# Splitting the projection weights on POOL alone instead of on ScalarE and VectorE, in a bidirectional hybrid mixer

## The chip, the core and the metric

The kernel runs on one core of one Trainium2 chip. The time is device microseconds of one execution. Of the core's engines, PE (TensorE) multiplies matrices, PEld is its weight load, DVE is VectorE, ACT is ScalarE, POOL is GpSimd, and SP issues most DMAs.

## The reference, cut to what matters

Two layers run over 256 context tokens and 1024 latent tokens, 1024 features wide. In each layer one input projection feeds three head groups, and one output projection closes the layer:

```python
h = _rmsnorm(x, g) * (1.0 + scale) + shift
proj = jnp.einsum('bld,de->ble', h, w_in)              # 4400 columns
(aq, ak, av, ao, az, ag, bq, bk, bv, bz, cq, ck, cv, cz, clr) = split(proj)
ha = mlstm(aq, ak, av, gates ag) both directions        # group A, 4 heads x 128
hb = retention(bq, bk, bv) both directions              # group B, 4 heads x 64
hc = gla(cq, ck, cv, log_a from clr) both directions    # group C, 4 heads, 32 x 64
y = concat(head_rms(sigmoid(ao) * ha), head_rms(hb), head_rms(hc)) * hn_g * silu(concat(az, bz, cz))
x = x + gate * jnp.einsum('ble,ed->bld', y, w_out)
```

All data are float32. The mLSTM's gates `ag` pass through a log-sigmoid, running sums and running maxima over the tokens before anything of group A can use them.

## The kernel before, in words

**Projections.** PE multiplies float32 data as three products of a high part (`hi`, type fp32r) and a rest (`lo`): hi by hi, hi by lo, lo by hi (`TERMS`). The normed activations lie split in `hA` (six chunks of 128 tokens) and `hB` (four chunks), first the high part, then the rest. Each weight tile is 1024 columns by 128 partitions: it lands in one of two `raw` buffers by a DMA of 512 KB, and `split` (L410 to L417) makes `hi` and `lo` of it, each a ring of three buffers. ACT copies raw to `hi` (a cast, L415), and DVE subtracts `hi` from raw into `lo` (L416).

**Two kinds of projection.** `w_fm` takes 128 output features over all 8 slices of the input (its split is one piece of 1024 columns), and `mm_fm` (L454) runs 24 matmuls over each of three token blocks of 256, 512 and 512. `w_tm` takes 256 output features in two weight tiles (each split in four pieces of 256 columns), and `mm_tm` (L466) runs 24 matmuls for each of the ten token chunks, two chunks to one PSUM bank; `pj` has two banks. There are 44 tiles of the first kind and 36 of the second, 16 of them for the output projection. `gates_w` (L508 to L518) makes 6 more tiles for the columns of `cv`, `ag` and `clr`, used by `gates` (L534).

**Order of the work.** `ORDER` names the steps of each layer; all steps are issued in that order, and a list scheduler places every instruction on its engine from its own estimate of when each is ready. Projections carry a low priority (`late`), so they fill the PE's time between the small matmuls of the head groups. On the engine the order is then fixed: an instruction that waits holds up all that stand behind it.

**The start of a layer.** The steps begin with `g` (gates), then `v0`, `cq`, `ck` and `m` in layer 0 and `cq`, `v0`, `ck` and `m` in layer 1. `gates` transposes its results on PE (L543), and ACT adds a bias into `G` (L544). `mlstm_rows` (step `m`, from L546) takes `G` and runs a chain of small operations on 36 partitions, nearly all on DVE: a copy (L554), the log-sigmoid (L207 to L213), 20 running sums (L504), running maxima (L560, L562), subtractions (L568 to L591), and an exponential on ACT (L593). Its result goes back to PE for transposition (L603, then L598). Step `d` (`decays`, matmul L653) and group C (L780 on) follow.

**POOL** does little: the power -1/2 in each head's norm (L619, L1190, L356), some clearing (as L650 in `decays`), a masked copy (L818) and a few of the activations' rests (L401).

Of the kernel before, what the change touches and what calls it, by code (L numbers as in the profile page):

```python
# [10 lines left out]
F32 = mybir.dt.float32  # L11
# [4 lines left out]
ALU = mybir.AluOpType  # L16
# [72 lines left out]
def hybrid_step(ctx: ExitStack, tc: tile.TileContext, A, O):  # L89
    nc = tc.nc  # L90
    pe, dve, act, pool, sync = nc.tensor, nc.vector, nc.scalar, nc.gpsimd, nc.sync
# [41 lines left out]
    def v3(t, n):  # L133

        return t.rearrange("p (a n) -> p a n", n=n)
# [271 lines left out]
            f5.give(*xn)  # L407


    def split(raw, parts=1, cols=1024):  # L410
        hi, lo = hi_ring(), lo_ring()
        n = cols // parts
        for i in range(0, cols, n):
            e = slice(i, i + n)
            act.copy(hi[:, e], raw[:, e])  # L415
            dve.tensor_tensor(lo[:, e], raw[:, e], hi[:, e].bitcast(F32), ALU.subtract)  # L416
        return hi, lo  # L417

    def w_fm(src, c0):

        raw = raw_ring()
        sync.dma_start(v3(raw, P), src[:, c0:c0 + P].rearrange("(k p) n -> p k n", p=P))
        hi, lo = split(raw)
        return v3(hi, P), v3(lo, P)

    def w_tm(src, c0, ks=range(KT)):

        out = []
        for g in range(2):
            raw = raw_ring()  # L430
            i = 0
            while i < 4:
                k = ks[4 * g + i]
                n = 1
                while i + n < 4 and ks[4 * g + i + n] == k + n:
                    n += 1
                sync.dma_start(v3(raw, 256)[:, i:i + n, :],
                               src[k * P:(k + n) * P, c0:c0 + 256].rearrange("(k p) n -> p k n", p=P))
                i += n
            hi, lo = split(raw, 4)  # L440
            out.append((v3(hi, 256), v3(lo, 256)))
        return out
# [34 lines left out]
    def proj_feat(l, c0, scale=None):  # L477
        w = w_fm(A["w_in"][l], c0)
        t = f5()
        for b, (t0, n) in enumerate(BLK):  # L480
            ps = mm_fm(w, b)
            evac(t[:, t0:t0 + n], ps[:, :n], scale)
        return t
# [23 lines left out]
    def gates_w(l):  # L507

        src = A["w_in"][l].rearrange("(k p) n -> p k n", p=P)
        out = []  # L510
        for k in range(0, KT, 3):
            n = min(3, KT - k)
            raw = raw_ring()
            r = v3(raw[:, 0:912], 304)[:, 0:n, :]
            for d, c0, m in ((0, C_CV, 256), (256, C_AG, 16), (272, C_LR, 32)):
                sync.dma_start(r[:, :, d:d + m], src[:, k:k + n, c0:c0 + m])
            hi, lo = split(raw, 1, n * 304)
            out.append((v3(hi[:, 0:912], 304), v3(lo[:, 0:912], 304)))  # L518
        return out

# [677 lines left out]
    def gate_z(l, c0, kt, y=None):  # L1198

        w = w_fm(A["w_in"][l], c0)  # L1200
        for b, (t0, n) in enumerate(BLK):
            ps = mm_fm(w, b)
            th = (wk if y is None else rw)()[:, :n]
            act.activation(th, ps[:, :n], AF.Tanh, scale=0.5)
            dve.scalar_tensor_tensor(th, th, 1.0, ps[:, :n], ALU.add, ALU.mult)
            if y is None:
                yv = wk()[:, :n]
                sync.dma_start(yv, yd[kt, :, t0:t0 + n])
            else:
                yv = y[:, t0:t0 + n]  # L1210
            dve.scalar_tensor_tensor(yv, th, hgh[:, 8 * l + kt:8 * l + kt + 1], yv, ALU.mult, ALU.mult)
            if y is None:
                sync.dma_start(yd[kt, :, t0:t0 + n], yv)


    def layer(l, general, w):
# [7 lines left out]
        def step_g():  # L1224
            e["vc"], e["G"] = anchored(gates, l, gates_w(l) if l or general else w)
# [148 lines left out]
    def program(general):  # L1374
        w = None
        if general:
            for b in range(3):
                norm_h(0, b, load_x(b))
        else:
            halves = range(4), range(4, 8)  # L1380
            units = [f5(1024) for _ in range(6)]
            xn = [load_x(0)]
            modulation_pe(0, units, scz)
            modulation_pe(1024, units, scz)
            with tc.issue_after(adas[-1].ins):
                xn.append(load_x(1))
            for b in range(2):
                norm_h(0, b, xn[b], halves[0])
            modulation_pe(512, units, scz)
            modulation_pe(1536, units, scz)  # L1390
            f5.give(*units)
            with tc.issue_after(adas[-1].ins):
                w = gates_w(0)
                xn.append(load_x(2))
            for b in range(3):
                norm_h(0, b, xn[b], halves[1] if b < 2 else range(KT))
# [53 lines left out]
```

## Time and profile before

| what | value |
| --- | --- |
| median of three runs | 1653.74 us (1653.5 to 1653.74) |
| profiled execution, its own time | 1656.08 us |
| span of its trace | 1654.1 us |
| PE busy | 1588.9 us (96%), 10874 matmuls |
| DVE busy | 984.9 us (60%), 2516 instructions |
| ACT busy | 615.7 us (37%), 1605 instructions |
| POOL busy | 153.1 us (9%), 243 instructions |
| DMA engines, mean over 16 | some 34% of the span |

The profiled execution took 2.0 us more than its span, and 2.3 us more than the median of the timed runs. PE's busy time counts a matmul from its start to its modelled end, and matmuls overlap, so a busy PE can still issue below its peak rate.

### The profile page before, as it was taken

To read this page: it belongs to the slowest core of one execution; us is meant where nothing else is said; L and a number is where in the kernel's file an instruction comes from. 1 tells how busy PE (TensorE), PEld (TensorE's weight loads), DVE (VectorE), ACT (ScalarE), POOL (GpSimd) and SP (SyncE) were. 2 spreads that over 40 slices of the span, in tenths; PEclk is the share of its full clock that TensorE was granted. 3 is DMA by queue.
4 is the path that set the end of the run, shared out by engine and by line. 5 is a ranking of instruction groups with operands and counts; after the bars stand their busy time and mean duration, and the time that the engine had idled before them with its cause. 6 is when DMAs were issued, how large, how long until landed. Compare 5 with 4: busy or idle time off the path is not lost.

```text
span 1654.1 us, 28521 instructions
## 1 busy us (share of the span) xinstructions
PE 1588.9 (96%) x10874; PEld 1430.0 (86%) x10874; DVE 984.9 (60%) x2516; ACT 615.7 (37%) x1605; POOL 153.1 (9%) x243
## 2 busy tenths in 40 slices
PE   6889999999999999999999899999999999899997
PEld 2887879888989998889999777999988989888997
DVE  3576664677779855763455677454537633466545
ACT  5535423434112324342365453244411223434323
POOL 1200221101001101000021012100001100000001
PEclk9998999999999999999999999999999999999999
DMA  9211323544324433561141031423233232435203
GB/s 326 71 41 40 76 66 92 153 144 123 102 82 141 149 111 118 192 187 35 37 160 39 17 87 44 110 84 102 73 96 85 58 93 83 125 105 178 80 13 131
DMA packets 169312, 167.43 MB, mean 101 GB/s; under 512 B 19084, under 2 KB 144940, under 8 KB 169164
## 3 DMA queue, kind: packets, MB, share of 16 engines
q1 hardware_dynamic: 168992, 165.45, 33.5%
q8 instruction: 87, 1.43, 0.4%
q14 instruction: 61, 0.50, 0.1%
q10 hardware_dynamic: 172, 0.05, 0.0%
HBM read 129.49 MB, written 27.85 MB: 95 GB/s over the span
## 4 chain that ended last, share of the span: by engine, by line
PE 81%; DMA 7%; DVE 7%; ACT 3%; issue 1%; SPq 0%; POOL 0%; POOLq 0%; DVEq 0%; ACTq 0%
PE pj L454 32%; PE pj L466 26%; PE pj L534 3%; DMA rw<-rrow 2%; PE mx L827 2%; PE mx L1172 2%; PE mx L1121 2%; PE mx L1174 2%; DMA wk<-yd 1%; DVE f L504 1%; DMA f<-f 1%; PE mx L999 1%; PE mx L1042 1%; PE mx L1163 1%; PE mx L292 1%
## 5 line engine op out<-in xcount | busy, mean ns | idle before, releaser
L454 PE MATMUL pj<-hA,hi 128*128 128x256 f32 (+1 forms) x1408 | 369.4, 345 | 0.1
L466 PE MATMUL pj<-hi,hA 128*128 128x256 f32 x1728 | 343.9, 286 | 6.5 <-ACT f L473 2.4
L466 PEld LDWEIGHTS pj<-hi,hA 128*128 128x128 f32 x1728 | 274.7, 189 | 10.8 <-ACT f L473 3.2
L454 PEld LDWEIGHTS pj<-hA,hi 128*128 128x128 f32 x1408 | 242.2, 189 | 30.7 <-issue 2.3
L466 PE MATMUL pj<-hi,hB 128*128 128x256 f32 x1152 | 248.5, 289 | 6.8 <-ACT f L1087 4.4
L454 PE MATMUL pj<-hA,lo 128*128 128x256 f32 (+1 forms) x704 | 238.5, 343 | 0.5 <-DVE lo L416 0.5
L466 PE MATMUL pj<-lo,hA 128*128 128x256 f32 x864 | 236.6, 285 | 0.0
L454 PE MATMUL pj<-hB,hi 128*128 128x512 f32 x704 | 234.8, 403 | 1.7 <-ACT f L473 0.9
L466 PEld LDWEIGHTS pj<-hi,hB 128*128 128x128 f32 x1152 | 193.5, 192 | 9.6 <-ACT f L1087 4.9
L416 DVE TENSOR_TENSOR lo<-raw,hi 128x256 fp32r<-128x256 f32 (+2 forms) x194 | 119.3, 628 | 101.5 <-ACT hi L415 90.0
L466 PE MATMUL pj<-lo,hB 128*128 128x256 f32 x576 | 165.4, 288 | 0.0
L466 PEld LDWEIGHTS pj<-lo,hA 128*128 128x128 f32 x864 | 159.1, 189 | 0.0
L454 PEld LDWEIGHTS pj<-hB,hi 128*128 128x128 f32 x704 | 129.9, 189 | 33.1 <-issue 4.1
L415 ACT CAST hi<-raw 128x256 fp32r<-128x256 f32 (+2 forms) x194 | 107.5, 566 | 135.9 <-PE pj L454 99.1
L454 PEld LDWEIGHTS pj<-hA,lo 128*128 128x128 f32 x704 | 132.7, 189 | 16.2 <-issue 1.0
L454 PE MATMUL pj<-hB,lo 128*128 128x512 f32 x352 | 140.7, 400 | 0.0
L466 PEld LDWEIGHTS pj<-lo,hB 128*128 128x128 f32 x576 | 110.2, 192 | 0.4 <-issue 0.3
L310 DVE SCALAR_TENSOR_TENSOR f<-f,sc 128x256 f32<-128x256 f32 x224 | 96.1, 480 | 16.5 <-DMA f<-in_w_ada_dram 16.2
L473 ACT COPY f<-pj 128x256 f32<-128x256 f32 (+2 forms) x142 | 48.4, 389 | 103.5 <-PE pj L466 48.0
L351 ACT ACTIVATE rw<-f 128x256 bf16<-128x256 f32 (+1 forms) x90 | 43.3, 482 | 107.7 <-DVE f L1343 102.8
L1156 DVE SCALAR_TENSOR_TENSOR rw<-rw,ccol,cst 128x128 f32<-128x128 f32 x160 | 46.7, 347 | 57.1 <-DMA rw<-rrow 56.9
L454 PEld LDWEIGHTS pj<-hB,lo 128*128 128x128 f32 x352 | 66.4, 189 | 15.4 <-issue 1.3
(282 smaller groups left out, 2546.9 us busy)
## 6 DMA issues: line engine op xcount, KB each, us to landing
raw<-in_w_in_dram SPq DMA_DIRECT2D x64, 512.0 KB
f<-in_w_ada_dram SPq DMA_DIRECT2D x32, 384.0 KB
wk<-yd SPq DMA_DIRECT2D x48, 256.0 KB
rw<-rrow SPq DMA_DIRECT2D x40, 256.0 KB
rw<-wrow SPq DMA_DIRECT2D x40, 256.0 KB
f<-in_w_ada_dram SPq DMA_DIRECT2D x16, 512.0 KB
f<-in_x_sample_dram SPq DMA_DIRECT2D x16, 512.0 KB
raw<-in_w_out_dram SPq DMA_DIRECT2D x32, 256.0 KB
```

Of the source, the lines that this page charges most:

```text
L310: dve.scalar_tensor_tensor(acc[v], w, scv[:, k, v:v + 1], acc[v], ALU.mult, ALU.add)
L351: act.activation(rw().bitcast(BF16)[:, 0:x.shape[1]], x, AF.Square, accum_out=out)
L415: act.copy(hi[:, e], raw[:, e])
L416: dve.tensor_tensor(lo[:, e], raw[:, e], hi[:, e].bitcast(F32), ALU.subtract)
L454: pe.matmul(ps[:, :n], lhsT=w[wi][:, k, :], rhs=hblk(xi, k, b), start=(i == 0), stop=(i == 23))
L466: pe.matmul(pv[:, u, :], lhsT=hchunk(xi, k, c), rhs=w[e // 4][wi][:, e % 4, :], start=(i == 0), stop=(i == 23))
L473: act.copy(out, ps)
L534: pe.matmul(ps, lhsT=hchunk(xi, k, c), rhs=w[k // 3][wi][:, k % 3, :], start=(i == 0), stop=(i == 23))
L827: pe.matmul(sc[d][:, 256 * p:256 * p + 256], lhsT=k[p][h, s], rhs=qm[p][h, :, u, :], start=True, stop=True)
L1121: pe.matmul(U[d], lhsT=ks[:, d * P:(d + 1) * P], rhs=v[:, c, :], start=True, stop=True)
L1156: dve.scalar_tensor_tensor(r4[:, d, e, :], r4[:, d, e, :], ccol[:, c0 + e, d, hd:hd + 1], negm[d], ALU.add, ALU.min)
L1172: pe.matmul(po[:, d, :], lhsT=r4[:, d, e, :], rhs=v[:, c, :], start=True, stop=not inter)
```

## The change

`split` gets a new argument, `own`, which is true unless the caller says otherwise. With it, POOL makes both parts: a cast of raw into `hi` (L417) and the subtraction into `lo` (L418). `w_fm` now splits in four pieces of 256 columns, as `w_tm` did already. Only the six gate tiles of `gates_w` keep ACT and DVE (L420, L421). Five lines are added inside `split`, so every later line of the kernel has a number five higher: L454 becomes L459, L466 becomes L471, L543 becomes L548, L603 becomes L608.

```diff
-    def split(raw, parts=1, cols=1024):
+    def split(raw, parts=1, cols=1024, own=True):
+
         hi, lo = hi_ring(), lo_ring()
         n = cols // parts
         for i in range(0, cols, n):
             e = slice(i, i + n)
-            act.copy(hi[:, e], raw[:, e])
-            dve.tensor_tensor(lo[:, e], raw[:, e], hi[:, e].bitcast(F32), ALU.subtract)
+            if own:
+                pool.tensor_copy(hi[:, e], raw[:, e])
+                pool.tensor_tensor(lo[:, e], raw[:, e], hi[:, e].bitcast(F32), ALU.subtract)
+            else:
+                act.copy(hi[:, e], raw[:, e])
+                dve.tensor_tensor(lo[:, e], raw[:, e], hi[:, e].bitcast(F32), ALU.subtract)
         return hi, lo
...
-        hi, lo = split(raw)
+        hi, lo = split(raw, 4)
...
-            hi, lo = split(raw, 1, n * 304)
+            hi, lo = split(raw, 1, n * 304, own=False)
```

Since the scheduler orders every engine anew, the change also moves instructions that it does not name. On PE, at the start of layer 0, the last transpositions of the gates (L543, into `mx`) and the first matmuls of `v0` (L466) stand like this before, with the first L603 of step `m` at the end:

```order
L543 MATMUL mx_112<-cst,sm_86 128x128
L466 MATMUL pj_110<-hi_66,hA_106 128x256
...
L466 MATMUL pj_110<-hi_66,hA_106 128x256
L543 MATMUL mx_112<-cst,sm_83 128x128
L466 MATMUL pj_111<-hi_66,hA_106 128x256
...
L454 MATMUL pj_111<-hA_107,hi_68 128x256
L603 MATMUL mx_114<-cst,f_99 128x36 x4
```

Of the change, the same place (L548 and L471 are the same two lines, L608 is L603):

```order
L548 MATMUL mx_112<-cst,sm_86 128x128
L471 MATMUL pj_110<-hi_66,hA_106 128x256
L471 MATMUL pj_110<-hi_66,hA_107 128x256
L548 MATMUL mx_112<-cst,sm_83 128x128
L471 MATMUL pj_111<-hi_66,hA_106 128x256
...
L471 MATMUL pj_111<-hi_67,hB_109 128x256
L608 MATMUL mx_114<-cst,f_99 128x36 x4
```

Before, 25 projection matmuls stand between the two transpositions and 203 more (189 of `v0`, 14 of `cq`) ahead of L603. With the change these are 2 and 142, all of `v0`. At the same place of layer 1 the projection matmuls ahead of L603 go from 204 (72 of `cq`, 132 of `v0`) to 127 (72 of `cq`, 55 of `v0`).

On POOL, at the start of layer 0, before, the clearing of the gates' tiles (L539) is followed at once by the clearing of step `d` (L650):

```order
L539 MEMSET sm_86 128x128
L539 MEMSET sm_83 128x128
L650 MEMSET f_105 64x10
L650 MEMSET f_94 64x10 x2
L1099 COPY f_98<-vT 128x1
```

Of the change, the splits of the two tiles of `v0` (`hi_66`, `hi_67`) and of `cq` (`hi_68`) stand between them:

```order
L544 MEMSET sm_86 128x128
L544 MEMSET sm_83 128x128
L417 CAST hi_66<-raw_65 128x256 x4
L418 TENSOR_TENSOR lo_69<-raw_65,hi_66 128x256
L417 CAST hi_67<-raw_64 128x256 x4
L418 TENSOR_TENSOR lo_69<-raw_65,hi_66 128x256 x3
L418 TENSOR_TENSOR lo_70<-raw_64,hi_67 128x256 x4
L417 CAST hi_68<-raw_65 128x256 x4
L418 TENSOR_TENSOR lo_71<-raw_65,hi_68 128x256 x4
L655 MEMSET f_105 64x10
L655 MEMSET f_94 64x10 x2
```

These are 24 new POOL instructions while step `m` runs on DVE; at the same place of layer 1 there are 32 (`cq`, both tiles of `v0`, `ck`).

On DVE, in the chain of step `m` of layer 1, splits (L416) stand between its operations before:

```order
L416 TENSOR_TENSOR lo_71<-raw_64,hi_68 128x256 x2
L554 COPY f_100<-f_105 36x1280
L416 TENSOR_TENSOR lo_71<-raw_64,hi_68 128x256 x2
L207 SCALAR_TENSOR_TENSOR f_98<-f_100 36x1280
L209 TENSOR_SCALAR f_104<-f_98 36x1280
...
L504 SCALAR_TENSOR_TENSOR f_98<-ones,f_100 4x128
L416 TENSOR_TENSOR lo_69<-raw_65,hi_66 128x1024
L504 SCALAR_TENSOR_TENSOR f_98<-ones,f_100 4x128 x5
```

Of the change, the same chain stands without them, and otherwise in the same order:

```order
L405 TENSOR_TENSOR hB_109<-rw_77,hB_108 128x512
L559 COPY f_100<-f_105 36x1280
L207 SCALAR_TENSOR_TENSOR f_98<-f_100 36x1280
L209 TENSOR_SCALAR f_104<-f_98 36x1280
...
L509 SCALAR_TENSOR_TENSOR f_98<-ones,f_100 4x128 x6
```

Before, five splits (four of 256 columns, one of 1024) stand between L554 and the second L504; with the change none does.

## Rows read from the trace of the kernel before

**Rows 1.** The page: busy time by engine, and the chain that ended last.

```profile
PE 1588.9 (96%) x10874; PEld 1430.0 (86%) x10874; DVE 984.9 (60%) x2516; ACT 615.7 (37%) x1605; POOL 153.1 (9%) x243
...
PE 81%; DMA 7%; DVE 7%; ACT 3%; issue 1%; SPq 0%; POOL 0%; POOLq 0%; DVEq 0%; ACTq 0%
```

**Rows 2.** Busy time by stretch: length, PE, PEld, DVE, ACT, POOL, granted clock, DMA.

```profile
100.00:120.00 20.00, 15.91 (x133) 15.50 (x132) 19.67 (x36) 3.99 (x8) 0.00 (x0) 1.00 0.02 3
120.00:134.00 14.00, 14.00 (x52) 10.74 (x52) 1.75 (x12) 6.29 (x9) 0.33 (x3) 0.51 0.04 8
134.00:900.00 766.00, 754.27 (x5175) 682.07 (x5174) 501.89 (x1308) 284.28 (x768) 75.24 (x106) 1.00 0.37 110
930.00:935.00 5.00, 5.00 (x28) 4.93 (x29) 1.20 (x9) 2.33 (x2) 0.11 (x1) 0.50 0.07 12
935.00:1654.00 719.00, 695.37 (x4797) 630.79 (x4796) 386.87 (x1034) 253.04 (x684) 62.02 (x84) 0.99 0.30 89
```

**Rows 3.** PE's waits: total, times, longest, in us.

```profile
PE mx L603 <- ACT f L593: 7.2, 2, 3.7
...
PE pj L454 <- DVE lo L416: 0.5, 1, 0.5
```

**Rows 4.** The page's groups of the splits: busy, mean ns, idle before.

```profile
L416 DVE TENSOR_TENSOR lo<-raw,hi 128x256 fp32r<-128x256 f32 (+2 forms) x194 | 119.3, 628 | 101.5 <-ACT hi L415 90.0
...
L415 ACT CAST hi<-raw 128x256 fp32r<-128x256 f32 (+2 forms) x194 | 107.5, 566 | 135.9 <-PE pj L454 99.1
```

**Rows 5.** The chain in order of time: start, length, a long run of projections.

```profile
1539.64 77.19 PE pj L466 x644
```

**Rows 6.** Layer 0, from the gates to L603: start, length, engine, line.

```profile
86.92 0.22 ACT L542 COPY sm<-pj 128x32 f32<-128x32 f32 x1
...
89.41 0.27 PE L543 MATMUL mx<-cst,sm 128*128 128x128 f32 x1
...
90.28 0.68 ACT L544 ACTIVATE f<-mx,gb 128x512 f32<-128x512 f32 x1
...
90.41 1.23 DVE L416 TENSOR_TENSOR lo<-raw,hi 128x1024 fp32r<-128x1024 f32 x1 [3.57 <-ACT hi L415]
91.67 0.82 DVE L554 COPY f<-f 36x1280 f32<-36x1280 f32 x1
...
119.87 1.11 PE L603 MATMUL mx<-cst,f 36*128 36x36 f32 x10 [3.71 <-ACT f L593]
```

**Rows 7.** Layer 1, the same stretch.

```profile
895.11 0.22 ACT L542 COPY sm<-pj 128x32 f32<-128x32 f32 x1
...
899.72 0.82 DVE L554 COPY f<-f 36x1280 f32<-36x1280 f32 x1
900.58 0.76 DVE L416 TENSOR_TENSOR lo<-raw,hi 128x256 fp32r<-128x256 f32 x2
...
917.85 1.22 DVE L416 TENSOR_TENSOR lo<-raw,hi 128x1024 fp32r<-128x1024 f32 x1
...
929.96 1.28 PE L603 MATMUL mx<-cst,f 36*128 36x36 f32 x10 [3.47 <-ACT f L593]
```

**Rows 8.** POOL's groups nearest to the new ones, shapes apart.

```profile
L818 POOL TENSOR_SCALAR rw<-f,heads_of 128x256 f32<-128x256 f32 x20 | 23.0, 1158 | 81.1 <-DVE f L741 42.3 <-PE mx L827 38.7
...
L401 POOL TENSOR_TENSOR hA<-rw,hA 128x256 fp32r<-128x256 f32 x4 | 3.5, 885 | 22.3 <-ACT hA L400 22.3
...
L674 POOL MEMSET sta<- 128x256 f32 x6 | 1.9, 312 | 5.3 <-DMA out_dram<-sta 2.8 <-issue 1.8 <-POOL nout L1107 0.7
```

**Rows 9.** DVE and POOL beside each other in the timeline from 61.8 us.

```profile
62.23 3.35 DVE L405 TENSOR_TENSOR hB<-rw,hB 128x512 fp32r<-128x512 f32 x2
...
62.04 1.29 POOL L401 TENSOR_TENSOR hB<-rw,hB 128x512 fp32r<-128x512 f32 x1 [8.29 <-ACT hB L400]
...
63.58 1.45 POOL L401 TENSOR_TENSOR hB<-rw,hB 128x512 fp32r<-128x512 f32 x1
```

**Rows 10.** DVE's line L405: durations in ns, least, median, most.

```profile
L405 DVE TENSOR_TENSOR hB<-rw,hB x12: 674/683/1777, 59.6 to 881.6; 128x512 fp32r<-128x512 f32 x12
```

## The prediction

> **What bounds the kernel now.** The page comes first: PE is busy 96% of the span, and 81% of the chain that ended last is PE's own work, with DVE 7%, DMA 7% and ACT 3% [rows 1]. So the 1654.1 us are PE's work plus its idle time, 1654.1 - 1588.9 = 65.2 us. The busy time by stretch says where that idle time lies: 4.1 us in 100 to 120 us, 11.7 us in 134 to 900, 23.6 us in 935 to 1654 [rows 2]; the rest is the start of the program and the end of step `m` of layer 1. The reader should also see two odd stretches there: in 100 to 120 DVE is busy 19.67 of 20 us while POOL does nothing, and behind that PE's granted clock is 0.51 (120 to 134), as it is 0.50 in 930 to 935. That is the lower of its two levels, 1.2 GHz for 2.4.
>
> PE's waits name the place. The largest one is L603, the first PE step of `m` behind the DVE chain: twice, 3.7 us at most, 7.2 us in all, always for the exponential on ACT (L593) at the end of that chain. Matmuls that wait for a `lo` of the splits after the gates come to 0.5 us [rows 3]. So the splits as such hold PE up almost nowhere. The groups show the same from the other side: DVE spends 119.3 us in 194 of them and ACT 107.5 us, but ACT was idle 99.1 us ahead of its casts, waiting for a buffer that PE still read (L454), and DVE 90.0 us waiting for the cast [rows 4]. The splits run ahead of PE and stop at its pace.
>
> **What is removed.** Of the 194 tiles 188 leave ACT and DVE. By the groups' means that is 188 x 0.566 = 106 us from ACT and 188 x 0.628 = 118 us from DVE (a little less, as the gates' tiles are of the larger forms). I count this at nothing wherever PE is the limit: the cover is the matmuls of the tiles ahead in the ring of three; without that cover the price would be a tile's split on either engine, 1.2 us, at each of 188 tiles.
>
> **What is added.** 80 tiles in four quarters are 320 casts and 320 subtractions on POOL, 128x256 each. A cast there is not in the trace. It is bounded from below by a memset of the size, 0.31 us, and from above by L818, one input from SBUF with a factor, 1.16 us; I take 0.5, as a cast only moves data, as the memset does. The subtraction has a row of its own shape and types, L401: 0.885 us [rows 8]. A quarter is 1.385 us, a tile 5.5 us, all of it 320 x 1.385 = 443 us, so POOL goes from 153 to some 595 us. PE takes 0.12 us a matmul in a long run of projections (77.19 us for 644) [rows 5], so 72 matmuls for a tile of the first kind are 8.6 us and 120 for one of the second 14.4 us. POOL is fast enough by its sum (443 us spread over 1600), with little room at the first tiles of a layer, where three or four come at once.
>
> **Moved: the work ahead of L603.** This is the largest term. PE fills the time of `m`'s DVE chain with projection matmuls, and the order of the change leaves fewer of them ahead of that step. In layer 0 there were 25 + 203 from the first of the last two transpositions, and there are 2 + 142, so 84 fewer, 84 x 0.12 = 10.1 us. In layer 1 there were 204 and are 127: 77 x 0.12 = 9.2 us. Before, PE already ran dry there by 3.71 us [rows 6] and 3.47 us [rows 7]. So nothing else is left to do, PE stands idle that much longer, and the same matmuls come later: **+19.3 us**. They could be had back only where PE idles later on and these would be ready; I count nothing for that (a rival below).
>
> **The chain starts earlier: gain.** In layer 0 the last transposition waits behind 23 of those 25 matmuls: ACT finished its operand at 86.92 + 0.22 = 87.14, it started at 89.41, then L544 ran, and L554 stood behind a split of 1.23 us on DVE, to 91.67 [rows 6]. With the change it could start at some 87.2, L544 at 88.07 (0.87 behind it, as now), and L554 when that ends, at 88.8: -2.9 us. In layer 1 the same operand is ready at 895.11 + 0.22 = 895.33 and L554 starts at 899.72; with the same 0.87 and 0.68 us behind the operand that is 896.9, -2.8 us. The splits inside that chain, a pair of 256 columns (0.76 us) and one of 1024 (1.22 us), go as well; the first pair starts the moment L554 ends: -1.9 us [rows 7]. Sum **-7.5 us** (2.9 + 2.8 + 1.9, rounded).
>
> **The chain is stretched by POOL: loss.** In 100 to 120 DVE works alone [rows 2]. With the change POOL splits beside it. What that does is seen once: at 62.23 two L405 on DVE took 3.35 us, while POOL did two L401 of 1.29 and 1.45 us [rows 9]; two of them usually take 2 x 0.683 us [rows 10]. So 2.74 us of POOL cost DVE 1.98 us, 0.72 for one. The order puts 24 POOL instructions (12 subtractions) into the chain's time in layer 0 and 32 (16) in layer 1; the first tile's casts will be done before the chain starts, and I estimate 11 and 12 subtractions behind that. The bounds are 0 (POOL works in DVE's gaps; there are hardly any) and the whole time of the casts too. Nearest are the rows named, subtractions of the same kind on both engines: (11 + 12) x 0.885 x 0.72 = **+14.6 us**. Casts I count at nothing, as they have one input, unlike the instructions of those rows.
>
> The Trainium skill (SBUF — State Buffer, section "SBUF: two separate sides") says that DVE and GpSimd share a pair of ports as an exclusive lock: a DVE instruction with two SBUF inputs and a GpSimd one that reads SBUF block each other for the whole instruction. The rows above agree as far as they go. By that rule the casts would count too, and all of the time.
>
> **Elsewhere.** The same stretching takes place on other DVE chains, and POOL's powers for the norms now stand behind splits that can wait for a ring buffer. Against that, DVE and ACT are freer. In 134 to 900 PE idles 11.7 us in all and in 935 to 1654 23.6 us, in many small waits [rows 2]. I set loss and gain equal, 0, with bounds of -10 and +15 us.
>
> **Sum.** 19.3 - 7.5 + 14.6 = +26.4 us. The profiled execution's own time was 1656.08, 2.0 us over its span and 2.3 us over the median; the change of the span is taken over to the median: 1653.7 + 26.4 = **1680 us**.
>
> **Rivals.** (a) *Faster.* The deferred 161 matmuls fill idle time further on. For it: 11.7 + 23.6 us of PE's idle time lie behind the two places, and projections are the filler. Against it: those waits are short and many stand ahead of work that has no filler ready, and the order of PE is fixed. If all 11.7 and half of 23.6 us were filled, 19.3 would be more than repaid (-23.5), and with the chain 7.5 us shorter and no stretching the time is 1653.7 + 19.3 - 23.5 - 7.5 = 1642 us. It decides from the point where more than 11.8 us of later idle time is filled, and DVE isn't stretched. (b) *No stretching.* POOL and DVE get past each other: 1653.7 + 11.8 = 1665.5 us. Against it stand the 3.35 us [rows 9]. (c) *The whole lock.* Every POOL instruction that reads SBUF holds DVE up in full, casts too: 11 x 0.885 + 4 x 0.5 and 12 x 0.885 + 11 x 0.5, together 27.9 us instead of 14.6: 1693 us. This is what the section named above would make of it. (d) *Late weights.* The cast costs 1.16 us, a tile 8.2 us, near the 8.6 us that PE takes for one; with three late by some 4 us at the first tiles of both layers and at six changes of columns in the output projection, 8 x 3 us = 24 us are added: about 1704 us.
>
> **How the numbers follow.** My forecast with its neighbourhood (1668 to 1688, terms off by a half each) has 0.5, (b) 0.14, (c) 0.15, (d) 0.08, (a) 0.07, and 0.06 is left for a mixture of gains and losses that comes out near zero. The range from 1660 to 1698 leaves out (a), the mixture and most of (d), 2 in 10. A change of 0.2% is 3.3 us, about what a measurement of this kernel can tell from none. Slower by more: forecast, (b), (c), (d), 0.86 of the chance with a little off at the edge of (b), so 0.85; same 0.07; faster 0.08.
>
> **What would show it.** L608 should wait for L598's exponential 15 us or more in both layers; PE's idle time in 100 to 120 should grow by over 10 us, and the lower granted clock stand again behind it. The running sums (L509) and L213 to L596 should take longer where L418 runs beside them, and L418 about 0.9 us, L417 about 0.5. DVE and ACT should lose some 110 us each without PE gaining anything. I am wrong if L608 waits no longer than before, if waits of L459 and L471 for POOL's `hi` or `lo` are the largest group, or if PE's idle time behind 134 us falls by 10 us.

## The result, and the profile after

The changed kernel takes 1737.53 us (median of 4 runs, 1736.37 to 1741.77), the kernel before 1653.74: a ratio of 1.0512, with a 95% interval from 1.0493 to 1.053. That is 84 us slower, where 26 were forecast. The profiled execution took 1736.37 us, its span is 1734.5.

The page of the changed kernel, busy time by engine [rows 1]:

```profile
span 1734.5 us, 28789 instructions
...
PE 1602.1 (92%) x10874; PEld 1439.5 (83%) x10874; DVE 945.4 (55%) x2328; ACT 519.1 (30%) x1417; POOL 547.4 (32%) x883
```

PE's idle time goes from 65.2 to 1734.5 - 1602.1 = 132.4 us, and its 10874 matmuls are busy 13.2 us longer, as more of them ran at the lower clock (the granted clock is 0.974 in the mean, and was 0.987). So of the 80 us that the span grew, 67 are waiting.

PE's waits in the changed kernel, in total, times and longest [rows 3]:

```profile
PE mx L608 <- ACT f L598: 26.0, 2, 13.1
PE pj L459 <- POOL lo L418: 10.9, 1, 10.9
...
PE pj L459 <- ACT f L478: 7.7, 6, 3.5
PE pj L459 <- ACT f L480: 7.2, 1, 7.2
PE mx L320 <- DVE f L310: 5.9, 4, 3.9
...
PE mx L1199 <- DVE sm L1196: 5.0, 4, 2.3
```

L608 waits 26.0 us, 13 in either layer, where L603 waited 7.2: the place is the one that was forecast, the size a little less (15 us or more in each). Below it stand waits that were hardly there: one of 10.9 us for a `lo` of POOL, and one of 7.2 us for L480, ACT's copy of a finished projection out of PSUM.

The busy time by stretch, columns as in [rows 2], step `m` of layer 0 in the first row and the end of that of layer 1 in the fourth:

```profile
100.00:120.00 20.00, 7.09 (x58) 6.68 (x56) 19.70 (x34) 3.10 (x6) 3.38 (x5) 0.75 0.11 28
...
134.00:900.00 766.00, 724.13 (x4909) 652.11 (x4908) 461.04 (x1181) 210.74 (x603) 247.17 (x385) 0.98 0.36 104
...
960.00:985.00 25.00, 12.15 (x74) 10.75 (x72) 18.63 (x34) 5.26 (x5) 3.35 (x7) 0.66 0.19 47
985.00:1734.00 749.00, 709.19 (x4868) 641.79 (x4867) 361.81 (x950) 209.49 (x604) 230.67 (x372) 0.99 0.29 85
```

In the two long stretches away from step `m` PE now idles 41.9 and 39.8 us, where it was 11.7 and 23.6 [rows 2]. This is what the forecast lacks. Set against PE's work done (its matmuls' columns summed in order, and the two traces compared where the sums are equal), the changed kernel is 22 us behind at 200 us of the kernel before, 30 at 480, 47 at 880, 66 at 920, 72 at 1000 and 79 at 1640: two steps at the starts of the layers, and a slope between them.

POOL's and DVE's groups of the changed kernel (busy, mean ns) [rows 4, 8]:

```profile
L418 POOL TENSOR_TENSOR lo<-raw,hi 128x256 fp32r<-128x256 f32 x320 | 259.5, 826 | 9.9 <-PE pj L459 2.9 <-PE pj L471 0.8
L417 POOL CAST hi<-raw 128x256 fp32r<-128x256 f32 x320 | 148.1, 477 | 474.1 <-PE pj L459 237.7 <-PE pj L471 197.2 <-DMA raw<-in_w_in_dram 20.9
...
L509 DVE TENSOR_TENSOR_SCAN f<-ones,f 128x129 f32<-128x129 f32 (+2 forms) x80 | 42.0, 589 | 0.4
```

The prices are those that were estimated (0.477 for 0.5 us, 0.826 for 0.885). But DVE lost only 984.9 - 945.4 = 39.5 us of busy time, where the splits that left it had taken some 118. Its other 2322 instructions, each counted from its own start to its end, take 1052.1 us in sum for 991.3 before: they became **61 us longer**. (Neighbours on DVE overlap a little, in both kernels alike, so these sums exceed the busy time.) Of the 61 us, 58 lie in the 1144 instructions that read two inputs from SBUF. The 760 that read one input from SBUF and one from PSUM take 285 us as before. Two lines of the same shape show it (`mx` is a PSUM tile, `f` lies in SBUF), and the running sums, which are L504 before and L509 now. Before:

```profile
L1164 DVE TENSOR_TENSOR rw<-rw,mx 128x512 f32<-128x512 f32 x40 | 27.2, 682 | 10.0 <-PE mx L1163 9.4
L1159 DVE TENSOR_TENSOR rw<-rw,f 128x512 f32<-128x512 f32 x40 | 27.2, 690 | 12.7 <-DMA rw<-wrow 8.9 <-ACT f L473 3.5
L504 DVE TENSOR_TENSOR_SCAN f<-ones,f 128x129 f32<-128x129 f32 (+2 forms) x80 | 26.6, 399 | 0.4
```

With the change (the running sums stand above, 589 ns for 399):

```profile
L1164 DVE TENSOR_TENSOR rw<-rw,f 128x512 f32<-128x512 f32 x40 | 29.6, 754 | 27.7 <-ACT f L478 15.6 <-DMA rw<-wrow 12.1
L1169 DVE TENSOR_TENSOR rw<-rw,mx 128x512 f32<-128x512 f32 x40 | 27.2, 682 | 10.9 <-PE mx L1168 10.0 <-ACT rw L1163 0.6
```

Step `m` of layer 0, from the timeline: DVE, then POOL beside it, then PE.

```profile
88.76 0.94 DVE L559 COPY f<-f 36x1280 f32<-36x1280 f32 x1 [20.05 <-ACT f L549]
89.73 1.90 DVE L207 SCALAR_TENSOR_TENSOR f<-f 36x1280 f32<-36x1280 f32 x1
...
99.46 6.54 DVE L509 TENSOR_TENSOR_SCAN f<-ones,f 36x128 f32<-36x128 f32 x13
...
87.59 7.28 POOL L418 TENSOR_TENSOR lo<-raw,hi 128x256 fp32r<-128x256 f32 x7
94.82 5.34 POOL L417 CAST hi<-raw 128x256 fp32r<-128x256 f32 x4
100.12 3.26 POOL L418 TENSOR_TENSOR lo<-raw,hi 128x256 fp32r<-128x256 f32 x4
...
120.71 1.28 PE L608 MATMUL mx<-cst,f 36*128 36x36 f32 x10 [13.12 <-ACT f L598]
```

The chain starts at 88.76 for 91.67 and takes 31.95 us to L608 for 28.20 [rows 6]; some 15 of the 24 splits run beside its first 15 us (the others were done before), and then POOL has no split until 143 us.

### The profile page after: what moved, and what is told of

Same layout as the page of the kernel before. It is cut to its first block, busy times and chain, and to the rows that moved or that the text cites. A ratio compares the mean times of both kernels' runs of the same rounds, so it can differ in the third digit from the quotient of the medians.

```text
span 1734.5 us, 28789 instructions
## 1 busy us (share of the span) xinstructions
PE 1602.1 (92%) x10874; PEld 1439.5 (83%) x10874; DVE 945.4 (55%) x2328; ACT 519.1 (30%) x1417; POOL 547.4 (32%) x883
## 4 chain that ended last, share of the span: by engine, by line
PE 62%; DVE 12%; DMA 10%; ACT 2%; issue 2%; POOL 1%; SPq 0%; POOLq 0%; DVEq 0%; ACTq 0%
PE pj L459 25%; PE pj L471 23%; DMA rw<-rrow 3%; DMA f<-in_w_ada_dram 3%; DVE f L310 2%; PE mx L1126 2%; DMA wk<-yd 2%; PE pj L539 2%; PE mx L1177 1%; DVE rw L1161 1%; PE mx L832 1%; DMA rw<-wrow 1%; PE mx L1179 1%; PE mx L1047 1%; PE mx L1004 1%
## 5 line engine op out<-in xcount | busy, mean ns | idle before, releaser
L459 PE MATMUL pj<-hA,hi 128*128 128x256 f32 (+1 forms) x1408 | 372.6, 347 | 18.2 <-POOL lo L418 10.9
L471 PE MATMUL pj<-hi,hA 128*128 128x256 f32 x1728 | 351.1, 290 | 12.9 <-DVE wk L1345 3.4
L417 POOL CAST hi<-raw 128x256 fp32r<-128x256 f32 x320 | 148.1, 477 | 474.1 <-PE pj L459 237.7
L471 PEld LDWEIGHTS pj<-hi,hA 128*128 128x128 f32 x1728 | 278.7, 192 | 21.0 <-DVE wk L1345 5.5
L459 PEld LDWEIGHTS pj<-hA,hi 128*128 128x128 f32 x1408 | 244.8, 192 | 51.0 <-POOL lo L418 11.3
L418 POOL TENSOR_TENSOR lo<-raw,hi 128x256 fp32r<-128x256 f32 x320 | 259.5, 826 | 9.9 <-PE pj L459 2.9
L471 PE MATMUL pj<-hi,hB 128*128 128x256 f32 x1152 | 243.1, 286 | 7.0 <-ACT f L1092 4.5
L459 PE MATMUL pj<-hB,hi 128*128 128x512 f32 x704 | 237.7, 406 | 10.7 <-ACT f L480 7.2
L459 PE MATMUL pj<-hA,lo 128*128 128x256 f32 (+1 forms) x704 | 238.8, 346 | 0.0
L471 PE MATMUL pj<-lo,hA 128*128 128x256 f32 x864 | 236.4, 288 | 1.2 <-POOL lo L418 1.2
L471 PEld LDWEIGHTS pj<-hi,hB 128*128 128x128 f32 x1152 | 189.9, 189 | 9.9 <-ACT f L1092 4.9
L459 PEld LDWEIGHTS pj<-hB,hi 128*128 128x128 f32 x704 | 131.1, 191 | 41.2 <-ACT f L480 8.1
L471 PEld LDWEIGHTS pj<-lo,hA 128*128 128x128 f32 x864 | 160.4, 192 | 2.3 <-POOL lo L418 1.8
L471 PE MATMUL pj<-lo,hB 128*128 128x256 f32 x576 | 162.1, 285 | 0.0
L459 PEld LDWEIGHTS pj<-hA,lo 128*128 128x128 f32 x704 | 134.2, 192 | 16.5 <-issue 2.0
L459 PE MATMUL pj<-hB,lo 128*128 128x512 f32 x352 | 141.5, 402 | 0.0
L310 DVE SCALAR_TENSOR_TENSOR f<-f,sc 128x256 f32<-128x256 f32 x224 | 103.5, 517 | 21.5 <-DMA f<-in_w_ada_dram 21.1
L471 PEld LDWEIGHTS pj<-lo,hB 128*128 128x128 f32 x576 | 108.2, 189 | 0.3 <-issue 0.3
L1345 DVE TENSOR_TENSOR wk<-pj,f 128x512 f32<-128x512 f32 (+1 forms) x45 | 28.1, 631 | 116.4 <-PE pj L471 115.7
L624 POOL TENSOR_TENSOR ti<-ti,mhalf 128x4 f32<-128x4 f32 x40 | 41.6, 1040 | 157.4 <-DVE ti L623 154.9
```

Of the source, the lines that this page charges most:

```text
L310: dve.scalar_tensor_tensor(acc[v], w, scv[:, k, v:v + 1], acc[v], ALU.mult, ALU.add)
L417: pool.tensor_copy(hi[:, e], raw[:, e])
L418: pool.tensor_tensor(lo[:, e], raw[:, e], hi[:, e].bitcast(F32), ALU.subtract)
L459: pe.matmul(ps[:, :n], lhsT=w[wi][:, k, :], rhs=hblk(xi, k, b), start=(i == 0), stop=(i == 23))
L471: pe.matmul(pv[:, u, :], lhsT=hchunk(xi, k, c), rhs=w[e // 4][wi][:, e % 4, :], start=(i == 0), stop=(i == 23))
L624: pool.tensor_tensor(ss, ss, mhalf[:, 0:4], ALU.pow)
```

## The experiments

Each was timed beside the kernel before on its own chip. The differences are of the medians; the intervals of the ratios are 0.2 to 0.35% (3 to 6 us) to either side. In the runs named `r_` the order of one or more engines is held to that of another kernel. Theories 1 to 3 are those that the expectation of `fill` names, A and B those of `r_after`.

| kernel | ratio | us over the kernel before |
| --- | --- | --- |
| the change | 1.0512 | +83.8 |
| fill | 1.0396 | +64.0 |
| poolq | 1.0463 | +74.7 |
| first | 1.0301 | +48.8 |
| subpool | 1.0251 | +41.2 |
| castpool | 1.0098 | +17.9 |
| quarters | 1.0184 | +31.0 |
| shadow | 1.0422 | +68.3 |
| bfill | 1.0080 | +14.2 |
| r_after | 1.0266 | +45.1 |
| r_before | 1.0407 | +67.2 |
| r_quarters | 1.0036 | +7.5 |
| r_cast | 1.0085 | +14.7 |
| r_sub | 1.0135 | +19.9 |
| r_shadow | 1.0858 | +140.8 |
| r_pe | 1.0459 | +74.5 |
| r_actdve | 1.0563 | +89.1 |

### Step m: fill, bfill and first

`fill` ties the transpositions of step `m` behind the end of `v0` in layer 0 and behind its sixth chunk in layer 1. `bfill` does the same in the kernel before.

`mms` lists the last projection matmul of each token chunk in `mm_tm`; the second set of transpositions is tied in the same way.

```diff
...
             for j in range(n):
-                pe.transpose(ps[:, j * P:(j + 1) * P], TR[:, (c0 + j) * P:(c0 + j + 1) * P], ident)
+                with tc.issue_after(mms[(-1, -5)[l]]):
+                    pe.transpose(ps[:, j * P:(j + 1) * P], TR[:, (c0 + j) * P:(c0 + j + 1) * P], ident)
...
```

Expected of `fill`: 

> The changed kernel, with the transpositions of step m (L608 and L603) tied behind later projection matmuls on PE: 262 and 259 projection matmuls stand ahead of them in the two layers, for 142 and 125. Theory 1 (PE runs dry at step m, because the order leaves too little work ahead of it): the wait of L608, 26.0 us in two, falls below 5 us and the time falls by 15 to 30 us, from 1737.5 to about 1712, as the lower clock behind the wait is rarer too. Theory 2 (the loss is that weights come late, because the splits on POOL queue behind instructions that wait): the wait moves to the projections further on, and the time falls by less than 8 us. Theory 3 (the loss is that POOL stretches DVE everywhere): 10 to 15 us, with DVE's busy time as it is.

It gained 20 us, inside theory 1's bounds for the time, but the wait did not go as theory 1 had it. PE's two largest waits in `fill`:

```profile
PE pj L473 <- ACT f L481: 23.4, 7, 11.1
PE pj L459 <- ACT f L483: 13.8, 3, 8.8
```

and ACT's timeline there, with PE's wait:

```profile
99.98 1.20 ACT L481 COPY f<-pj 128x256 f32<-128x256 f32 x4 [3.39 <-PE pj L473]
117.15 1.28 ACT L601 ACT_TABLE_LOAD   x1 [15.97 <-DVE ti L584]
118.44 1.27 ACT L601 ACTIVATE f<-f 36x1280 f32<-36x1280 f32 x1
...
122.19 1.20 ACT L481 COPY f<-pj 128x256 f32<-128x256 f32 x4
...
122.89 0.80 PE L473 MATMUL pj<-hi,hB 128*128 128x256 f32 x2 [10.56 <-ACT f L481]
```

PE had more projections ahead of step `m` and yet stood still for 10.56 us: `pj` has two banks, and the copies that free them (L481) stand on ACT behind the exponential at the end of the chain. So work ahead of the wait is of use only as far as ACT stands in the same order.

Expected of `bfill`: 

> The kernel before, with the transpositions of step m tied behind later projection matmuls on PE: 239 and 238 stand ahead of them, for 203 and 181. If PE's waits of 3.7 and 3.5 us there and the lower clock behind them (some 9 us of matmuls at half speed, twice) are what they seem, the time falls by 7 to 15 us. If the deferred step only makes others wait further on, it is unchanged within 4 us or longer.

It is 14 us slower (ratio 1.0054 to 1.0106): the second expectation. Of PE's waits of 3.7 and 3.5 us at step `m` one of 1.9 us is left, but others came: the largest group is now L785, which is L780 of the kernel before, for group C's product on DVE, 8.1 us in three where it was 3.1 in two. So the step behind `m` seems as urgent as what was put ahead of it.

`first` splits the tiles of `v` of group A, `cq` and `ck` on ACT and DVE again:

```diff
-            hi, lo = split(raw, 4)
+            hi, lo = split(raw, 4, own=own)
...
-        w = w_tm(A["w_in"][l], c0)
+        w = w_tm(A["w_in"][l], c0, own=c0 != C_AV)
```

Expected: 

> The changed kernel with the tiles of both v steps of group A, of cq and of ck on ACT and DVE as before, all others on POOL. 203 and 183 projection matmuls stand ahead of step m again. Theory 1: L608 waits 7 us in all as before, and the time falls to about 1710, some 27 us. Theory 2: 10 us or less from the start of layer 1 (the split behind L823 is of a later tile), so 1727 or more. Theory 3: about a sixth of DVE's stretching goes, and the time falls by some 10 us.

It gained 35 us, more than any theory had. L608 waits 6.8 us in two, as before. The rest of the loss, 49 us, is not at step `m`.

### POOL's queue: poolq

```diff
-                pool.tensor_scalar(t[:, 0:256], x, heads_of[:, 0:1], None, ALU.mult)
+                act.activation(t[:, 0:256], x, AF.Copy, scale=heads_of[:, 0:1])
```

Expected: 

> The changed kernel with the masked copy of group C (L823) on ACT and no longer on POOL, so that no split of weights stands behind it. Theory 2: the wait of 10.9 us for POOL's lo at 1028 us goes or falls below 3 us, and the time falls by 8 to 15 us. Theory 1: unchanged within 4 us, with L608 waiting 26 us still. Theory 3: at most 3 us, for POOL's 19 us of L823.

The wait of 10.9 us had this cause in the changed kernel's timeline (POOL, then PE):

```profile
1020.50 4.91 POOL L418 TENSOR_TENSOR lo<-raw,hi 128x256 fp32r<-128x256 f32 x6
1034.92 1.84 POOL L823 TENSOR_SCALAR rw<-f,heads_of 128x256 f32<-128x256 f32 x2 [9.50 <-DVE f L746]
1036.70 1.44 POOL L417 CAST hi<-raw 128x256 fp32r<-128x256 f32 x4
1038.10 0.73 POOL L418 TENSOR_TENSOR lo<-raw,hi 128x256 fp32r<-128x256 f32 x1
...
1038.95 0.77 PE L459 MATMUL pj<-hA,hi 128*128 128x256 f32 x2 [10.88 <-POOL lo L418]
```

L823 waits 9.50 us for group C's product, the next tile's splits stand behind it, and PE waits for the first of them. With L823 on ACT that wait is gone from PE's list, and the loss is 74.7 us for 83.8, 9 us less, as theory 2 said. The intervals of the two ratios touch, so the 9 us are less sure than that the wait is gone. It explains this one wait and no more.

### One half of the split on POOL, or neither: subpool, castpool, quarters

`subpool` casts on ACT and subtracts on POOL (its edit is shown), `castpool` casts on POOL and subtracts on DVE, `quarters` casts on ACT and subtracts on DVE, so that only the quarters are left of the change.

```diff
-                pool.tensor_copy(hi[:, e], raw[:, e])
+                act.copy(hi[:, e], raw[:, e])
```

Expected of `subpool`: 

> The changed kernel with only the subtractions on POOL, the casts on ACT (in quarters). 211 and 144 projection matmuls stand ahead of step m. Theory 3, with the subtraction as what blocks DVE: DVE's other instructions stay longer by some 45 us of the 60, and the time falls by less than 15 us. Theory 1: layer 0 gets its 8 us back and layer 1 about 2, so 1727. Theory 2: POOL has 148 us less in its queue, but a lo still stands behind L823, so no change of more than 5 us.

Of `castpool`: 

> The changed kernel with only the casts on POOL, the subtractions on DVE (in quarters). 212 and 187 projection matmuls stand ahead of step m. With the casts harmless to DVE (as the prediction had it): DVE's instructions keep their times within 15 us in all, and the time is within 10 us of the kernel before. With the casts blocking as much as their time: about 25 us of stretching, and 15 to 25 us more than before.

Of `quarters`: 

> The changed kernel with casts on ACT and subtractions on DVE again, so that only the splitting of the first kind of tiles into quarters is left of the change. All theories: within 5 us of the kernel before; more would make the quarters themselves a cause.

`subpool` gained 43 us, more than any theory allowed. `castpool`, at 18 us, has the time of its second expectation but the DVE of its first: DVE's instructions other than splits take 999.5 us for 991.3, 8 us longer and not 25. `quarters` was a surprise: without a single split on POOL it costs 31 us. So the comparison of such variants mixes two things, what the engines do and how the scheduler orders everything for it. All readings above carry that doubt; the runs named `r_` hold the order.

### POOL's work with its results unused: shadow

```diff
+        for i in range(0, cols if cols == 1024 else 0, 256):
+            x = raw[:, i:i + 256]
+            pool.tensor_copy(x, x)
+            pool.tensor_tensor(x, x, hi[:, i:i + 256].bitcast(F32), ALU.subtract)
```

Expected: 

> The kernel before, where the splits stay on ACT and DVE, and POOL does the same 320 pairs once more in place on raw, behind them (a copy and a subtraction of 128x256 each), which nothing uses. PE, DVE and ACT keep all that they had, and 214 and 178 projection matmuls stand ahead of step m, for 203 and 181 before. So what it costs is POOL's use of the shared memory ports and of its own queue, without the weights depending on POOL. Theory 3 (stretching of DVE): DVE's instructions become longer by 50 to 70 us in all, and the time rises by 25 to 45 us. Theories 1 and 2: the time stays within 8 us of the kernel before.

It costs 68 us: theory 3 by its sign, beyond its bounds, and again with a new order. DVE's instructions other than splits take 1062.0 us, 71 more than before. The run leaves out less than it says: as POOL works on `raw` in place, the next load of that buffer has to wait for POOL (see `r_shadow`).

### The order held: r_after and r_before

These kernels take the order of each engine from another kernel's program, as lists of indices, and chain the instructions by edges that order and do not wait; the splits and POOL are left free. The traces show the orders as meant, instruction by instruction, on PE, DVE and ACT.

```diff
+    def replay(engine, packed):
...
+        order = struct.unpack(f"<{len(b) // 2}H", b)
+        mine = [i for i in nc.cur_bb.bb.instructions if i.engine == engine and i.name not in free]
+        for a, b in zip(order, order[1:]):
+            tc.add_manual_dep(mine[b], mine[a].name, mybir.DependencyInfo(
+                mybir.DependencyClass.NoSync, mybir.DependencyReason.DATA), reason="replay")
...
```

Expected of `r_after`: 

> The changed kernel with its splits on POOL as they are, and every other instruction of PE, DVE, ACT and SP in exactly the order of the kernel before (edges of order alone, no waits). So PE has 203 and 181 projection matmuls ahead of step m again, and the new order is gone from the change. Theory A (the new order is the larger part of the loss): the time falls to 1650 to 1680 us. Theory B (POOL's stretching of DVE is the larger part): it stays above 1690.

Of `r_before`: 

> The other half: the splits on ACT and DVE as before (whole tiles of the first kind), placed freely, and every other instruction of PE, DVE, ACT and SP in exactly the order of the changed kernel. POOL has none of the new work. Theory A: above 1690, with waits of L603 of some 9 us each, as the order has only 142 and 125 projection matmuls ahead of it, and the chain isn't stretched. Theory B: below 1680.

In the order of the kernel before, the change costs 45 us; the order of the changed kernel without any of its work on POOL costs 67. `r_before` came out as theory A said, with its waits at step `m`, and `r_after`, at 1698.7 us, as theory B said. So both causes are real, and they do not add up (45 + 67 is more than 84). The order in `r_before` was made for an ACT and a DVE without these splits, which they do here, so a part of the 67 us may be that it does not suit them. Two pairs hold the work and change nothing but the order: the change and `r_after` (84 and 45 us), and `quarters` above and `r_quarters` below (31 and 7.5). There the new order costs 39 and 23 us. `r_before`, PE's waits:

```profile
PE mx L608 <- ACT f L598: 20.7, 2, 11.3
PE pj L459 <- ACT f L480: 12.6, 4, 8.2
```

and ACT there, then PE:

```profile
1012.15 1.36 ACT L743 ACTIVATE f<-f,taus 128x1280 f32<-128x1280 f32 x1 [6.29 <-DVE f L746]
1013.42 0.89 ACT L824 ACTIVATE rw<-f,heads_of 128x256 f32<-128x256 f32 x2
...
1016.41 1.05 ACT L480 ACTIVATE f<-pj 128x512 f32<-128x512 f32 x2
...
1017.04 0.80 PE L459 MATMUL pj<-hA,hi 128*128 128x256 f32 x2 [8.21 <-ACT f L480]
```

The copy of a finished projection stands behind L743, which waits for DVE, and PE stops when both banks are full. In the kernel before, the waits of PE for these copies (L473, L475) are 1.4 us at most, the longest in this group:

```profile
PE pj L466 <- ACT f L473: 4.5, 7, 1.4
```

L608 has 13.5 us of the 67. PE's other waits, summed over the trace, grew by 19 us for these copies and by 16 us for DVE, and its matmuls are busy 11 us longer.

`r_after` has hardly a wait for a split (PE for POOL's `lo`: 2.7 us in 7), so weights are not late in that order. It has DVE's stretching. The page of `r_after`, and its running sums (L504 of the kernel before):

```profile
PE 1608.7 (95%) x10874; PEld 1444.3 (85%) x10874; DVE 950.3 (56%) x2328; ACT 521.9 (31%) x1417; POOL 557.0 (33%) x883
```

```profile
L514 DVE TENSOR_TENSOR_SCAN f<-ones,f 128x129 f32<-128x129 f32 (+2 forms) x80 | 37.0, 528 | 0.4
```

DVE's instructions other than splits take 1055.4 us, 64 more than the 991.3 before, in the same order; 62 of the 64 lie in those with two inputs from SBUF. PE's idle time is 1697.5 - 1608.7 = 88.8 us, 24 more, and its matmuls are busy 19.8 us longer. The granted clock is 1.00 from 940 to 950 us and falls at the waits that follow:

```profile
950.00:960.00 10.00, 3.89 (x34) 0.84 0.04 6
960.00:970.00 10.00, 10.00 (x55) 0.82 0.05 9
...
1020.00:1030.00 10.00, 8.26 (x29) 0.66 0.02 3
```

(Columns: length, PE's busy time and matmuls, granted clock, DMA's share and GB/s.) So here the waits cost themselves and nearly as much again in matmuls at the lower level of the clock.

### Which order: r_pe and r_actdve

Expected of `r_pe`: 

> The kernel before, with only PE's instructions in exactly the order of the changed kernel (142 and 125 projection matmuls ahead of step m); ACT, DVE, POOL and SP are placed freely to suit. If the loss of the new order is PE's alone: 40 us or more over the kernel before, of the 67 us that the order of all four engines took. If it is that ACT and DVE stand in an order that doesn't suit: below 25 us.

Of `r_actdve`: 

> The kernel before, with the instructions of DVE and ACT other than the splits in exactly the order of the changed kernel, PE, POOL, SP and the splits placed freely to suit (167 and 127 projection matmuls ahead of step m). If the loss of the new order is PE's alone: below 25 us over the kernel before, most of it at step m. If it lies in the order of ACT and DVE: 40 us or more.

Both are beyond 40 us (75 and 89), so the loss is not in the order of one engine alone. Each alone costs what the whole order costs, or more: the likely reason is that engines wait for each other where one is held to an order that the others do not share.

### The parts of the split in one order: r_quarters, r_cast, r_sub, r_shadow

Expected of `r_quarters`: 

> Splits of the first kind of tiles in quarters, on ACT and DVE, and every other instruction of PE, DVE, ACT and SP in exactly the order of the kernel before. With the order free the quarters alone took 30 us more. If that was the new order: within 5 us of the kernel before now. If it was the 132 more instructions on ACT and on DVE: 15 us or more over it.

Of `r_cast`: 

> Casts on POOL and subtractions on DVE, in quarters, and every other instruction in exactly the order of the kernel before. With the order free this took 16 to 18 us more than the kernel before. If the casts alone block DVE: 10 us or more over it still. If that was order: within 5 us of it, or faster, as ACT is freer.

Of `r_sub`: 

> Casts on ACT (in quarters), subtractions on POOL, and every other instruction in exactly the order of the kernel before. If POOL's subtractions stretch DVE and the casts do not: 30 us or more over the kernel before, most of the 44 us of all splits on POOL in this order. If each costs by its time on POOL: some 25 to 30 us, as the casts on POOL took 14.

The quarters cost 7.5 us (ratio 1.0019 to 1.0053), between their two expectations, so some 23 of their 31 were the new order. Casts on POOL cost 15, subtractions on POOL 20 (both with the quarters in them), casts and subtractions together 45. The running sums (399 ns before) in `r_sub`:

```profile
L512 DVE TENSOR_TENSOR_SCAN f<-ones,f 128x129 f32<-128x129 f32 (+2 forms) x80 | 34.3, 494 | 0.4
```

The same of `r_cast`, and the subtractions, which DVE kept there:

```profile
L512 DVE TENSOR_TENSOR_SCAN f<-ones,f 128x129 f32<-128x129 f32 (+2 forms) x80 | 28.1, 417 | 0.3
...
L420 DVE TENSOR_TENSOR lo<-raw,hi 128x256 fp32r<-128x256 f32 x320 | 138.3, 449 | 100.1 <-POOL hi L418 94.7 <-PE pj L462 2.5 <-PE pj L474 1.4
```

DVE's instructions other than splits take 1038.4 us in `r_sub`, 47 more than before, 998.8 in `r_cast`, 8 more, and 992.2 in `r_quarters`, 1 more. It is mostly POOL's subtraction that stretches DVE. The cast adds little, though it holds up the subtractions on DVE as well (138.3 us, and 128.9 in `r_quarters`). Whether the second input or the longer time (0.74 us for 0.39 where DVE is idle) makes the difference was not tried. So `r_cast` has the time of its first expectation, but not for the reason given there; what makes up its 15 us beyond the 7.5 of the quarters was not settled. `r_sub`, at 20 us, lies below both of its expectations; its rows speak for the first.

Expected of `r_shadow`: 

> The kernel before in exactly its own order on PE, DVE, ACT and SP, splits on ACT and DVE, and POOL doing the 320 pairs once more behind them, in place on raw, unused. It rose by 70 us where the order was free. Theory A: most of that came with the new order, so now less than 25 us over the kernel before. Theory B: 40 us or more over it, at the same order.

It costs 141 us, twice what it costs with the order free (68). Theory B by its bound, but this is not the price of DVE's stretching, which is less here than in `r_after` (52 us for 64, splits left out). The next load of a `raw` buffer waits on SP for POOL's work in place, and ACT's casts wait for the loads, 44.6 us where it was 6.7 before:

```profile
SPq L427 <- POOL raw L421: 279.7, 42, 38.9
```

```profile
ACT hi L416 <- DMA raw<-in_w_in_dram: 44.6, 7, 9.4
```

How the 141 us divide between these waits and the stretching was not tried. What the pair shows on order is that the old one does not always lose less: here the free order costs half as much, while for the change itself it was the worse one (84 for 45).

## Why the prediction was wrong

**What bounds the kernel; the splits as such hardly hold PE up.** Right. In the held order PE waits 2.7 us for POOL's `lo`.

**What is removed.** Counted at nothing, and no run shows a gain from it. But two readings are off. The 194 and 188 are split instructions and not tiles: the 80 tiles that moved had 188 of them (44 of 1024 columns, 144 of 256). And DVE lost 39.5 us of busy time and ACT 96.6, where some 110 each were to be the sign.

**What is added.** Right: 408 us on POOL for 443. But 8.6 us for PE's work on a tile of the first kind is too short, as 48 of its 72 matmuls have 512 columns. In the trace before, these follow each other every 0.23 us, not 0.12, which makes some 14 us, so PE's work covers more of a split than rival (d) says.

**The work ahead of L603, the chain's earlier start and its stretching.** Right in kind, somewhat too large. L608's waits grew by 18.8 us where the three terms sum to 26.4 (the gain of the earlier start is 2.9 + 2.8 + 2.0 = 7.7, not 7.5, which changes nothing). PE's idle time in 100 to 120 us grew by 8.8 us, where over 10 were to be the sign. The start came 2.9 us earlier in layer 0, as worked out. The chain became 3.75 us longer in layer 0 (31.95 for 28.20), and in layer 1, from L559 at 943.44 to L608 at 977.67, 34.23 us for 30.24 - 1.98 = 28.26 without the splits that left it: 6.0. Together 9.7 us for the 14.6 forecast: POOL subtracted for some 22 us beside the two chains, so 0.44 us for each of them and not 0.72. That the casts count for little was right too (`r_cast`), so the whole lock of rival (c) did not come.

The Trainium skill (SBUF — State Buffer, section "SBUF: two separate sides") has DVE's instructions with two SBUF inputs and POOL's that read SBUF block each other in full. `r_sub` agrees in kind: with 320 subtractions, 260 us on POOL, DVE's other instructions take 47 us more, 45 of them in those with two SBUF inputs. `r_cast` shows far less: with 162 us of casts, which read SBUF too, they take 8 us more.

**Elsewhere, loss and gain equal, 0.** This is the step that failed. Of the 80 us by which the span grew, 19 are L608's waits, and 13 are matmuls at the lower clock all over the kernel; 48 are waits elsewhere, where the bound was 15. Of these, PE waited 17 us more for DVE, 14 for the copies out of PSUM on ACT, 12 for POOL's splits and 4 for other work of ACT. Two causes stand in the place of that step.

First, the new order was read at step `m` and POOL's places alone, but it holds for all 1650 us: with the same work it costs 39 us (the change against `r_after`), and without any of that work on POOL 67 us (`r_before`), of which L608 has 13.5. One kind of place is a copy out of PSUM that stands on ACT behind an instruction that waits for DVE.

Second, DVE's stretching, 61 us, was priced beside two chains (14.6 us) and set against gains everywhere else; with the order held, POOL's work costs 45 us (`r_after`) with 2.9 us of them in the waits at step `m` (10.1 us for 7.2). That the stretching is the whole of these 45 us is not shown: `r_sub` has 47 of its 64 us and loses 20. POOL's powers for the norms, which the prediction named here, were not held up: in `r_after` POOL stood waiting for the operand ahead of 85 of the 95, for 88 before.

And waits were counted at their length: the lower clock behind them takes a fifth as much again in the changed kernel (13 us for 67), and nearly as much again in `r_after` (20 for 24).

**Rivals.** (a) was excluded: nothing that was deferred was had back. (b) did not come, as the chain is 9.7 us longer. (d), late weights, came to 12.4 us, nearly all at one place, and there not by POOL's speed but by its queue (10.9 us; `poolq` has some 9 back).

**Left open.** How the 84 us divide between the order and POOL's work has no single answer, as the parts do not add: taken one way it is 45 for the work and 39 for the order on top of it (`r_after`), taken the other way 67 for the order and 17 for the work (`r_before`). What the 45 us hold beside DVE's stretching is open. Why the new order is so poor, when the scheduler made it to suit its own estimates, was not tried.

## What to carry to other kernels

Where a scheduler places everything from estimates, an edit in one helper re-orders every engine, and that can cost more than the edit: here 23 us for splitting a tile into quarters, which cost 7.5 in the old order. Measure an edit with the old order held as well, and compare the orders of all engines, over the whole kernel, not only where the largest wait stands. Subtractions moved to POOL were paid by those instructions of DVE that read two inputs from SBUF; those with one of them in PSUM stayed as they were. And work that PE needs soon must not stand in POOL's queue behind instructions that wait for another engine.

## What was unexpected of the hardware

POOL's cast of 128x256 and its subtraction of the same size act quite differently on DVE: 320 of each, 162 and 260 us on POOL, made DVE's other instructions 8 and 47 us longer; both together made them 64 longer, a little more than the sum. Where one of the two inputs of a DVE instruction lies in PSUM, nothing was added in any of these runs. In the chain of layer 0 it was POOL's casts that gave way: four of them took 5.34 us beside DVE's log-sigmoid, and 1.57 us a few microseconds earlier, when DVE was idle.
